# Hybrid attention layer: where the filler matmuls of the output projection start and stop, and when the first head's tiles are loaded

## The chip, the cores and the metric

One core of one Trainium2 chip runs the program. The metric is the device time of one launch in microseconds, the median over runs. Before the change three runs took 2358.67, 2354.69 and 2355.07 us, so the median is 2355.07 us. Lower is better.

## The reference

One layer with a learned prefix of 16 meta tokens ahead of 2048 tokens of width 1024 (2064 rows in all). A layer norm comes first. One input projection gives q, k and v of 16 heads of width 64, a forget logit per head, a gate for attention, a pool input and a gate for the pool branch. Attention is causal, with a bias from a running sum of log-sigmoids:

```python
log_f = jax.nn.log_sigmoid(f_logit + b_forget)
c = jnp.cumsum(log_f, axis=1)
s = q @ k.T * HEAD_DIM ** -0.5 + c[t] - c[s]
p = jax.nn.softmax(where(causal, s, -inf))
a = (p @ v) * jax.nn.silu(g_att)
p = multiscale_pool(u, w_pool, pool_scale) * jax.nn.silu(g_pool)
y = jnp.concatenate([a, p], axis=-1) @ w_out
out = layer_norm(ALPHA * x + y)
```

The output projection `w_out` has 2048 input rows, the first 1024 for the attention branch and the last 1024 for the pool branch, and 1024 output columns. The output drops the 16 meta rows. All of it is float32; the kernel gets the precision by splitting operands in a high and a low part and adding three products.

## The kernel before, in words

The program has three stages. In the first (lines 189 to 710) the rows are normalised, transposed and kept in SBUF, and a list of jobs (lines 657 to 668) projects them: `qk_job` for a head's q and k, `gp_job` and `u_job` for the pool branch, `ga_job` for the attention gate. A job makes its result in tiles, each of 24 matmuls (`proj`, line 490), in the two PSUM buffers of `dense` (line 169). `ga_job` (line 599) makes four tiles of 512 tokens; for each, ScalarE writes silu of the tile to `gst` (line 602), which has a single SBUF buffer, and a transfer stores it to `gd` in device memory. Everything but the last of these jobs runs before the attention pools are opened; the last one (`run_jobs(drain, len(jobs))`, line 796) is the `ga_job` of column block 7, and runs after they are opened.

The second stage is attention (lines 713 to 1103). The order of heads and query chunks is `seqn`: for each head the four chunks `j` of 512 queries, and for the last two heads the chunks 3, 0, 1, 2 in turn. Each (head, chunk) is cut in units: one per full key tile of 128 keys, and two more for the ragged end (`units`, line 895), so 3, 7, 11 and 15 units for the four chunks and 576 in all. The loop over `m` (lines 1080 to 1099) writes out, for each unit: `emit_s` (scores `s` on TensorE in one of four PSUM buffers; two exponentials on ScalarE, to `ph` in SBUF and back to `s`; pair sums `tu` and `acc` on GpSimd), then filler matmuls, then `emit_pl` (VectorE: `pl`, the low part of the exponential, and the running sum `acc`), and with a lag of four units `emit_pv` (products `xo` and `yo` with v). Each engine runs its instructions in the order in which they are written out here.

The filler is the output projection (`out_proj`, line 871): 32 tiles of the pool half, 16 with the first 512 output columns and 16 with the second, and then four `EARLY` tiles (12 to 15) of the attention half. Each tile is 24 matmuls `d<-wh,xm` and `d<-wl,xm` in one PSUM buffer (line 848), with its rows `xm` in one of two buffers. `out_tiles` is a generator that yields 1 after a matmul and 0 where it has to wait for something (line 835). Line 1079 gives the bounds: from unit `LEAD` = 24 to the last but `TAIL` = 24 the 768 matmuls of the pool half are spread over the units by weight; after that up to four are taken per unit. What is left then runs behind the loop (line 1100).

Every second unit calls `service` (line 1060): it takes one task of `wtasks`, which loads one of eight weight blocks (`wo_task`, line 825; `wst` has four buffers), and three rounds later splits it: `wh` on ScalarE, `wl` on VectorE (`wo_split`, line 814). It also runs the steps that are due for finished chunks (`chunk_end`, line 909: reciprocal, gate, store to `xa`).

The keys, values and queries come from device memory. `load_kv` (line 744) loads a quarter of a head's k and v in four transfers (`ka`, `kb`, `vt`, `vc`), `load_q` (line 760) a chunk of q in three (`qa` twice, `qb`). Ahead of the last job only the first quarter of head 0 and the first chunk are asked for (lines 792 to 795); `prefetch` (line 777) asks for the others from within the loop. All transfers are issued by SyncE, in one order that a scheduler sets; it may move a transfer ahead of others, and each waits at the head of the queue until its data and its buffer are free.

The third stage (lines 1105 to 1169) does the rest of the attention half of the projection and the closing layer norm, with its own buffers for the rows; the first two row tiles still come through the two `xm` buffers of the second stage (`first_x`, line 880).

Of the kernel before, what the change touches and what calls it, by code (L numbers as in the profile page):

```python
# [40 lines left out]
def kernel(  # L41
# [20 lines left out]
    nc = tc.nc  # L62
# [35 lines left out]
    nc = NC()  # L98
    mm = nc.tensor.matmul

    def dma(out, in_):
        out, in_ = out[tuple(slice(None) for _ in out.shape)], in_[tuple(slice(None) for _ in in_.shape)]
        nc.sync.dma_start(
            out.bitcast(F32) if out.dtype == F32R else out, in_.bitcast(F32) if in_.dtype == F32R else in_
        )
# [6 lines left out]
    def split(hi, lo, src, lo_eng=None):  # L112
        nc.scalar.copy(out=hi, in_=src)
        (lo_eng or nc.vector).tensor_tensor(out=lo, in0=src, in1=f32(hi), op=ALU.subtract)
# [18 lines left out]
    def pool(stack, name, **k):  # L133
        if k.get("space") is not DRAM:
            k["reuse_waits"] = "tile"
        return stack.enter_context(tc.tile_pool(name=name, bufs=1, **k))
# [535 lines left out]
    def fetch(n):  # L672
        return w_load(jobs[n][2]) if n < len(jobs) else None

    cur = w_first
    state = {"st": fetch(1)}
# [6 lines left out]
    def run_jobs(n0, n1):  # L683
        for n in range(n0, n1):
            fn, a, _ = jobs[n]

            def mid():
                if n + 1 < len(jobs):
                    state["w"] = w_split(state["st"])
                    state["st"] = fetch(n + 2)  # L690

            w = state.get("w") or cur
            if fn is not qk_job:
                m = n
                steps = 0
                while m < len(jobs) and jobs[m][0] is not qk_job and m != drain:
                    steps += 40 if jobs[m][0] is u_job else 32
                    m += 1
                sched["steps"] = steps if m == drain else steps + KT
                sched["tail"] = True  # L700
            fn(a, w, mid)
# [33 lines left out]
    NQ = 3  # L735
# [8 lines left out]
    def load_kv(h, i):  # L744
        ka, kb, (vt, vc) = kas[h % 2], kbs[h % 2], vts[h % 2]
        half, h8 = divmod(h, 8)
        if i == loaded[h]:
            loaded[h] += 1
            c0, c1 = 512 * i + (NM if i else 0), 512 * (i + 1) + NM
            dma(ka[2:68, c0:c1], kqd[h, 0:66, c0:c1])  # L750
            dma(kb[:, c0:c1], kqd[h, 2:130, c0:c1])
            dma(vt[:, 4 * i : 4 * i + 4, 0:P], vd[half][h8, :, 4 * i : 4 * i + 4, :])
            dma(vc[0:NM, i, 0:P], vd[half][h8, :NM, 4 * i + 4, :])
# [6 lines left out]
    def load_q(n):  # L760
        h, j = seqn[n]
        qa = qas[n % NQ]
        qb = kvs[0].tile([P, 512], F32R, tag="qb", name="qb", bufs=NQ)
        sl = slice(NM + 512 * j, NM + 512 * (j + 1))
        dma(qa[0:2, :], kqd[h, 258:260, sl])
        dma(qa[4:68, :], kqd[h, 194:258, sl])
        dma(qb, kqd[h, 130:258, sl])
        qt[n] = (qa, qb)
# [3 lines left out]
    kvq = deque()  # L772
    for n, (h, j) in enumerate(seqn):
        kvq.extend((h, i) for i in range(4) if i <= j and (h, i) not in kvq)
    fetched = [0]
# [13 lines left out]
            load_q(fetched[0])  # L789
            fetched[0] += 1  # L790

    load_kv(0, 0)
    load_q(0)
    fetched[0] = 1
    kvq.popleft()
    run_jobs(drain, len(jobs))
    phase_a.close()

# [1 line left out]
    bw = pool(phase_w, "bw", side="right")  # L800
# [8 lines left out]
    def wo_load(pl, half, n, k):  # L809
        st = pl.tile([P, 512], F32, tag="wst", name="wst", bufs=4)  # L810
        dma(st, wout[8 * half + k, :, 512 * n : 512 * (n + 1)])
        return st

    def wo_split(pl, half, n, k, st, eng=None):
        wh = pl.tile([P, 512], F32R, tag="wh", name="wh", bufs=KT)
        wl = pl.tile([P, 512], F32R, tag="wl", name="wl", bufs=KT)
        split(wh, wl, st, eng)
        wsl[half, n, k] = (wh, wl)
# [6 lines left out]
    def wo_task(args):  # L825
        def a():
            st = wo_load(bw, *args)
            todo_late.append((state["round"] + 3, lambda: wo_split(bw, *args, st, None)))

        return a  # L830

    wtasks = deque(wo_task((1, 0, k)) for k in range(KT))
    todo_late = deque()
# [221 lines left out]
                after(1, lambda: chunk_end(p, j))  # L1055

    total_fill = 2 * 16 * KT * 3
    nseq = len(seq)

    def service():  # L1060
        state["round"] += 1
        r = state["round"]
        while todo_late and todo_late[0][0] <= r:
            todo_late.popleft()[1]()
        if wtasks:
            wtasks.popleft()()
        due = sorted(t for t in post if t[0] <= r)
        for t in due:
            post.remove(t)
            t[2]()  # L1070
# [5 lines left out]
        n, i, u, nu = seq[m] if m < nseq else seq[-1]  # L1076
        return 2.0 if i < nu - 2 else 1.0

    LEAD, TAIL = 24, 24
    for m in range(nseq + LAG):  # L1080
        if m < nseq:
            emit_s(m)
        if m >= LEAD:
            if m < nseq - TAIL:
                w = [weight(t) for t in range(m, nseq - TAIL)]
                state["fill"] += (total_fill - filled[0]) * w[0] / sum(w)
            else:
                state["fill"] = 4.0
            k = min(int(state["fill"]), 4)
            state["fill"] = min(state["fill"] - k, 4.0)  # L1090
            fill(k)
        if m < nseq:
            emit_pl(m)
        if m >= LAG:
            emit_pv(m - LAG)
        if 0 < m < nseq:
            prefetch(seq[m][0], seq[max(m - LAG + 1, 0)][0])
        if m % 2:
            service()
    for r in filler:  # L1100
        if not r:
            service()
# [30 lines left out]
    for i in range(AHEAD - 1):  # L1133
        c_half(order[i], *tiles[i], 0)
        for k in range(KT * i // (AHEAD - 1), KT * (i + 1) // (AHEAD - 1)):
            wo_split(cp, 0, 1, k, sts[k])
            if k + WAHEAD < KT:
                sts.append(wo_load(bw, 0, 1, k + WAHEAD))
            service()
# [5 lines left out]
    for i, tt in enumerate(order):  # L1145
        if i + AHEAD < 16:
            c_half(order[i + AHEAD], *tiles[i + AHEAD], 0)
        xs, yt, st = tiles[i]
# [80 lines left out]
```

## Time and profile before

| what | value |
|---|---|
| median of three runs | 2355.07 us (2354.69 to 2358.67) |
| the profiled execution | 2353.42 us, span 2351.7 us, mean granted clock of TensorE 0.994 |
| TensorE matmuls | busy 2289.3 us (97%), 11450 instructions |
| VectorE, ScalarE, GpSimd | busy 1501.9, 959.9 and 716.8 us |
| first stage, attention, third stage | to 1320.45 us, to 2169.1 us, to the end |
| first and last filler matmul in the attention loop | at 1358.57 us and about 2167 us |

Times in the profile are counted from the start of the span. Busy time of TensorE holds matmuls that overlap: a 512-column matmul is listed with 0.39 us, but the next one starts 0.23 us after it when nothing waits. So a stretch in which TensorE lost time is seen better by the matmuls that it started per microsecond than by its busy share. Line L86 is a helper through which every instruction is recorded; the tile names tell the instructions apart.

### The profile page before, as it was taken

What the parts mean: (1) busy time and instruction counts of PE and PEld (TensorE: products, weight loads), DVE (VectorE), ACT (ScalarE), POOL (GpSimd) and SP (SyncE); (2) the same over time, 40 slices, a digit from 0 to 9 for tenths busy, and PEclk for the clock granted to TensorE, in tenths of its full rate; (3) what the DMA queues carried; (4) which work ended last, traced back from release to release, by engine and by line L of the source; (5) the groups of instructions that cost most, each with busy time, mean ns of one, the idle gap of its engine ahead of it and who ended that gap; (6) DMA issues with size and microseconds to landing.
All of it is one profiled execution on the core that took longest, in us unless ns stands there. A gap on an engine that the chain in (4) does not pass through costs nothing.

```text
span 2351.7 us, 32595 instructions
## 1 busy us (share of the span) xinstructions
PE 2289.3 (97%) x11450; PEld 1924.1 (82%) x11450; DVE 1501.9 (64%) x2372; ACT 959.9 (41%) x1813; POOL 716.8 (30%) x528
## 2 busy tenths in 40 slices
PE   6999999999999999999999999999999999998998
PEld 5878799999999999999888677777777777776787
DVE  6641146755766567656634488778788878877357
ACT  4431221212212212121111587777778777776000
POOL 4740021212313414140001235444453544444000
PEclk8999999999999999999999999999999999999999
DMA  7853222222222222222212857566666667555965
GB/s 252 265 175 90 69 90 70 84 63 92 91 62 91 78 70 91 62 95 80 82 65 71 219 170 226 162 210 175 186 189 187 208 173 228 169 164 164 300 193 165
DMA packets 317507, 333.59 MB, mean 142 GB/s; under 512 B 27744, under 2 KB 241072, under 8 KB 317312
## 3 DMA queue, kind: packets, MB, share of 16 engines
q1 hardware_dynamic: 317344, 331.51, 46.2%
q8 instruction: 91, 1.49, 0.3%
q14 instruction: 72, 0.59, 0.1%
HBM read 207.43 MB, written 124.00 MB: 141 GB/s over the span
## 4 chain that ended last, share of the span: by engine, by line
PE 89%; DVE 3%; DMA 3%; ACT 2%; issue 2%; POOL 1%; SPq 0%; DVEq 0%; ACTq 0%; POOLq 0%
PE d L86 61%; PE s L86 11%; PE yo L86 7%; PE mx L86 6%; PE xo L86 5%; POOL tu L86 1%; DVE pl L86 1%; PE tr L86 1%; ACT ph L86 1%; POOL araw L86 1%; DMA wst<-in_wout_dram 0%; ACT s L86 0%; DMA wu<-in_wut_dram 0%; DMA g_bc<-in_ln_in_g_dram 0%; DVE acc L86 0%
## 5 line engine op out<-in xcount | busy, mean ns | idle before, releaser
L86 PE MATMUL d<-hh,wh 128*128 128x412 f32 (+2 forms) x1472 | 543.8, 369 | 0.0
L86 PE MATMUL d<-hl,wh 128*128 128x412 f32 (+2 forms) x1472 | 538.2, 366 | 0.0
L86 PE MATMUL d<-hh,wl 128*128 128x412 f32 (+2 forms) x1472 | 537.9, 365 | 0.0
L86 DVE TENSOR_TENSOR pl<-s,ph 128x512 fp32r<-128x512 f32 (+2 forms) x576 | 375.4, 664 | 147.0 <-ACT s L86 134.2
L86 DVE TENSOR_REDUCE mxs<-mx 128x1 f32<-128x912 f32 (+14 forms) x416 | 359.5, 865 | 85.6 <-PE mx L86 75.8
L86 ACT ACTIVATE ph<-s 128x512 fp32r<-128x512 f32 (+2 forms) x576 | 335.2, 582 | 170.1 <-PE s L86 157.8
L86 PE MATMUL d<-wh,xm 128*128 128x512 f32 x1024 | 352.1, 400 | 4.5 <-DMA xm<-xa 3.7
L86 ACT ACTIVATE s<-s 128x512 f32<-128x512 f32 (+2 forms) x576 | 332.7, 578 | 0.0
L86 PEld LDWEIGHTS d<-hl,wh 128*128 128x128 f32 x1472 | 277.6, 189 | 24.8
L86 PEld LDWEIGHTS d<-hh,wh 128*128 128x128 f32 x1472 | 276.8, 188 | 23.2
L86 PEld LDWEIGHTS d<-hh,wl 128*128 128x128 f32 x1472 | 276.6, 188 | 23.4
L86 PE MATMUL s<-qa,ka 68*128 68x512 f32 (+4 forms) x704 | 257.9, 367 | 19.1 <-DVE pl L86 18.8
L86 POOL TENSOR_TENSOR wl<-wst,wh 128x1024 fp32r<-128x1024 f32 x40 | 96.3, 2407 | 571.4 <-ACT wh L86 545.8
L86 PE MATMUL s<-qb,kb 128*128 128x512 f32 (+4 forms) x704 | 244.8, 351 | 0.0
L86 PE MATMUL xo<-ph,vt 128*128 128x512 f32 (+3 forms) x640 | 232.7, 367 | 0.0
L86 POOL TENSOR_TENSOR tu<-ph 128x512 f32<-128x512 f32 x144 | 191.2, 1330 | 135.3 <-ACT ph L86 118.8
L86 PEld LDWEIGHTS d<-wh,xm 128*128 128x128 f32 x1024 | 192.3, 189 | 42.3 <-issue 2.9
L86 PE MATMUL yo<-pl,vt 128*66 128x512 f32 (+3 forms) x640 | 223.3, 365 | 1.1 <-ACT c L86 1.1
L86 PE MATMUL d<-wl,xm 128*128 128x512 f32 x512 | 204.3, 399 | 0.0
L86 PE MATMUL mx<-ka,qa 66*128 66x512 f32 (+5 forms) x704 | 197.9, 347 | 3.4 <-ACT qa L86 3.4
L86 PEld LDWEIGHTS s<-qa,ka 68*128 68x128 f32 (+1 forms) x704 | 127.8, 182 | 73.3 <-DVE pl L86 31.1
L86 DVE TENSOR_TENSOR mx<-mx,mask_q 128x128 f32<-128x128 f32 x256 | 76.6, 299 | 117.4 <-PE mx L86 115.0
(140 smaller groups left out, 3091.5 us busy)
## 6 DMA issues: line engine op xcount, KB each, us to landing
xm<-xp SPq DMA_DIRECT2D x32, 1024.0 KB
xm<-xa SPq DMA_DIRECT2D x20, 1024.0 KB
vd<-vs SPq DMA_DIRECT2D x32, 512.0 KB
vt<-vd SPq DMA_DIRECT2D x64, 256.0 KB
qb<-kqd SPq DMA_DIRECT2D x64, 256.0 KB
xa<-am SPq DMA_DIRECT2D x32, 512.0 KB
xp<-pm SPq DMA_DIRECT2D x32, 412.0 KB
kqd<-lo SPq DMA_DIRECT2D x64, 206.0 KB
```

Source lines behind the costliest of these rows:

```text
L86: return in_order(f(*a, **k))
```

## The change

Four edits. `LEAD` and `TAIL` go from 24 and 24 to 14 and 8. All four quarters of head 0 and the first three chunks of q (`NQ` is 3) are loaded ahead of the last projection job. In the first eight rounds of `service` two weight tasks are taken per round. The blocks that these tasks load are split two rounds later, with `wl` on GpSimd.

```diff
-    load_kv(0, 0)
-    load_q(0)
-    fetched[0] = 1
-    kvq.popleft()
+    for i in range(4):
+        load_kv(*kvq.popleft())
+        if i < NQ:
+            load_q(i)
+    fetched[0] = NQ
     run_jobs(drain, len(jobs))
     phase_a.close()
...
             st = wo_load(bw, *args)
-            todo_late.append((state["round"] + 3, lambda: wo_split(bw, *args, st, None)))
+            d, eng = (2, nc.gpsimd) if state["round"] < 8 else (3, None)
+            todo_late.append((state["round"] + d, lambda: wo_split(bw, *args, st, eng)))
...
     total_fill = 2 * 16 * KT * 3
+    LEAD, TAIL = 14, 8
     nseq = len(seq)
...
-        if wtasks:
-            wtasks.popleft()()
+        for _ in range(2 if r < 8 else 1):
+            if wtasks:
+                wtasks.popleft()()
...
-    LEAD, TAIL = 24, 24
     for m in range(nseq + LAG):
```

On SyncE, at the last projection job, the transfers stood like this before (`gd<-gst` is the store of a gate tile, the others are loads for attention):

```order
L86 DMA qa<-kqd 64x512
L86 DMA qb<-kqd 128x512
L86 DMA gd_68<-gst 128x512
L86 DMA ka<-kqd 66x512
L86 DMA kb<-kqd 128x512
L86 DMA vt<-vd_58 128x4x128
L86 DMA gd_68<-gst 128x512
L86 DMA vc<-vd_58 16x128
L86 DMA qa<-kqd 2x512
```

and now like this:

```order
L86 DMA qa<-kqd 64x512
L86 DMA qb<-kqd 128x512
L86 DMA ka<-kqd 66x512
L86 DMA kb<-kqd 128x512
L86 DMA vt<-vd_58 128x4x128
L86 DMA vc<-vd_58 16x128
L86 DMA gd_68<-gst 128x512 x3
L86 DMA wst<-in_wout_dram 128x512
L86 DMA gd_68<-gst 128x512
```

The first store of the job stood behind seven of the attention loads and now stands behind 25, and two more stores follow it directly.

On ScalarE, in the first units of attention, a weight cast (`wh<-wst`) stood between the exponentials (`ph`, `s`) of two units:

```order
L86 COPY c_10556<-yo 65x512
L86 ACTIVATE ph<-s 128x512
L86 ACTIVATE s<-s 128x512
L86 CAST wh<-wst 128x512
L86 ACTIVATE ph<-s 128x400
L86 ACTIVATE s<-s 128x400
L86 ACTIVATE ph<-s 128x432
L86 ACTIVATE s<-s 128x432
L86 CAST wh<-wst 128x512
```

and now two stand together, four times over:

```order
L86 COPY c_10578<-yo 65x512
L86 ACTIVATE ph<-s 128x512
L86 ACTIVATE s<-s 128x512
L86 CAST wh<-wst 128x512 x2
L86 ACTIVATE ph<-s 128x400
L86 ACTIVATE s<-s 128x400
L86 ACTIVATE ph<-s 128x432
L86 ACTIVATE s<-s 128x432
L86 CAST wh<-wst 128x512 x2
```

All eight casts now stand ahead of the exponentials of unit 12; before, three of them did.

On TensorE, behind the last score matmuls of attention, filler stood between the last products before (`d<-wh,xm` is a matmul of the first `EARLY` tile):

```order
L86 MATMUL s<-qa,ka 16x16
L86 MATMUL s<-qb,kb 16x16
L86 MATMUL d<-wh,xm 128x512 x2
L86 MATMUL d<-wl,xm 128x512
L86 MATMUL d<-wh,xm 128x512
L86 MATMUL xo<-ph,vt 128x512
L86 MATMUL yo<-pl,vt 66x512
L86 MATMUL d<-wh,xm 128x512
```

and now none does:

```order
L86 MATMUL s<-qa,ka 16x16
L86 MATMUL s<-qb,kb 16x16
L86 MATMUL xo<-ph,vt 128x512
L86 MATMUL yo<-pl,vt 66x512
L86 MATMUL xo<-ph,vt 128x512
L86 MATMUL yo<-pl,vt 66x512
L86 MATMUL xo<-ph,vt 128x512
L86 MATMUL yo<-ph,zo 66x512
```

All four `EARLY` tiles now stand behind the last product of attention, where three stood. The pool half of the filler now ends at unit 567 of 575. Before, it ended at unit 552, the units 553 to 572 had no filler, and the first `EARLY` tile began at unit 573.

## Rows read from the trace of the kernel before

**Rows 1.** The page: busy time of TensorE; the chain that ended last, by engine.

```profile
PE 2289.3 (97%) x11450; PEld 1924.1 (82%) x11450; DVE 1501.9 (64%) x2372; ACT 959.9 (41%) x1813; POOL 716.8 (30%) x528
PE 89%; DVE 3%; DMA 3%; ACT 2%; issue 2%; POOL 1%; SPq 0%; DVEq 0%; ACTq 0%; POOLq 0%
```

**Rows 2.** Windows: length, busy us (instructions) by engine, TensorE clock, DMA share, GB/s.

```profile
1301.00:1313.00 12.00, 12.00 (x53) 9.76 (x52) 0.27 (x1) 1.20 (x2) 3.84 (x5) 1.00 0.83 226
1320.45:1358.57 38.12, 32.40 (x162) 22.66 (x160) 29.18 (x47) 33.76 (x67) 11.36 (x11) 0.91 0.96 262
1325.50:1332.30 6.80, 4.93 (x18) 3.68 (x17) 3.26 (x5) 5.82 (x12) 1.71 (x2) 0.50 1.02 276
1344.18:1358.57 14.39, 12.69 (x64) 8.31 (x62) 13.65 (x23) 14.39 (x30) 5.13 (x4) 1.00 0.86 249
1400.00:1700.00 300.00, 296.80 (x1576) 228.41 (x1575) 244.30 (x380) 232.91 (x445) 139.09 (x106) 1.00 0.64 190
2126.50:2158.00 31.50, 25.37 (x124) 18.00 (x123) 30.47 (x45) 25.37 (x51) 16.35 (x12) 0.95 0.69 200
2169.00:2190.75 21.75, 17.24 (x76) 13.35 (x74) 3.56 (x6) 2.67 (x5) 0.00 (x0) 1.00 0.90 268
2190.75:2340.00 149.25, 149.25 (x658) 123.57 (x659) 84.84 (x124) 8.18 (x20) 4.28 (x3) 1.00 0.71 224
```

**Rows 3.** Timeline of ScalarE, last job to unit 1: start, length, idle before, releaser.

```profile
1304.01 0.60 ACT L86 ACTIVATE gst<-d 128x512 f32<-128x512 f32 x1 [4.54 <-PE d L86]
1309.73 0.60 ACT L86 ACTIVATE gst<-d 128x512 f32<-128x512 f32 x1 [5.12 <-DMA gd<-gst]
1315.13 0.60 ACT L86 ACTIVATE gst<-d 128x512 f32<-128x512 f32 x1 [4.80 <-PE d L86]
1320.69 0.60 ACT L86 ACTIVATE gst<-d 128x512 f32<-128x512 f32 x1 [4.96 <-PE d L86]
1321.31 1.28 ACT L86 ACT_TABLE_LOAD   x1
...
1326.46 0.50 ACT L86 ACTIVATE ph<-s 128x400 fp32r<-128x400 f32 x1 [2.77 <-DMA gd<-gst]
```

**Rows 4.** Timeline of SyncE's queue: when a transfer was issued.

```profile
1301.12 0.37 SPq L86 DMA_DIRECT2D ka<-kqd  x1
...
1304.87 0.37 SPq L86 DMA_DIRECT2D gd<-gst  x1
...
1321.32 0.32 SPq L86 DMA_DIRECT2D gd<-gst  x1
...
2126.64 0.56 SPq L86 DMA_DIRECT2D rd<-st  x1
...
2129.05 1.27 SPq L86 DMA_DIRECT2D rb<-rd  x2
...
2175.95 0.57 SPq L86 DMA_DIRECT2D xm<-xa  x1
```

**Rows 5.** Chain of waits: pieces that are transfers (start, length).

```profile
1321.32 5.04 DMA gd<-gst
1327.34 4.56 DMA ka<-kqd
```

**Rows 6.** Timeline of ScalarE, first units of attention.

```profile
1328.14 0.60 ACT L86 ACTIVATE ph<-s 128x512 fp32r<-128x512 f32 x1
...
1329.13 0.61 ACT L86 ACTIVATE ph<-s 128x512 fp32r<-128x512 f32 x1
...
1342.99 0.62 ACT L86 CAST wh<-wst 128x512 fp32r<-128x512 f32 x1 [1.00 <-DMA wst<-in_wout_dram]
1343.51 0.59 ACT L86 ACTIVATE ph<-s 128x512 fp32r<-128x512 f32 x1
```

**Rows 7.** Timeline of TensorE: starts after a wait, and a gap.

```profile
1328.02 0.79 PE L86 MATMUL s<-qa,ka 68*128 68x512 f32 x1 [1.87 <-DVE pl L86]
...
2183.76 0.47 PE L86 MATMUL d<-wh,xm 128*128 128x512 f32 x1 [2.46 <-DMA xm<-xa]
```

## The prediction

> **What bounds the kernel now.** I read the page first: TensorE is listed busy for 97% of the span and holds 89% of the chain that ended last [rows 1]. So the time is TensorE's work, which the change does not alter (the same matmuls, in another order), plus the time in which TensorE waits. Then I read windows, to find where it waits. In the middle of attention it starts 1576 matmuls in 300 us, 5.25 per us; in the third stage, where all are 512 columns wide, 658 in 149.25 us, 4.41 per us [rows 2]. At these rates the other stretches show what they lose:
>
> - From the first score matmul to the first filler (1320.45 to 1358.57) there are 162 matmuls in 38.12 us. They need 162 / 5.25 = 30.9 us, so 7.3 us are lost. ScalarE is busy for 33.8 of them, and for all of the last 14.39 us [rows 2]: two exponentials per unit hold it for about 1.0 us (a pair begins at 1328.14, the next at 1329.13 [rows 6]), a full unit's four matmuls hold TensorE for 0.93.
> - From 2126.5 to 2158 (the units 553 to 572, which have no filler) there are 124 matmuls in 31.5 us; they need 23.6, so 7.9 are lost. VectorE is busy for 30.5 of them [rows 2].
> - From 2169.00 to 2190.75 three early tiles stand alone: 72 filler matmuls need 72 / 4.41 = 16.3 us of 21.75, so 5.4 are lost [rows 2], in waits for `xm` and the single accumulator (2.46 us is the longest [rows 7]).
>
> The sum of these, 20.6 us, is all that the change can win back; the rest of attention is bound by TensorE at either density of filler. Next I read ScalarE and SyncE's queue at the last projection job, because the change fills that queue [rows 3, 4].
>
> **The change part by part.** The sum is made against the profiled execution, 2353.42 us, which is 1.65 below the median of the runs, 2355.07.
>
> *Loads ahead of the last job's stores.* Before, seven loads took SyncE from 1301.12 to 1304.87, and the first gate store followed at once [rows 4]. It landed at 1309.73, 4.86 us later, when ScalarE could write `gst` again [rows 3]. Now 25 loads go first. The first seven take 3.75 us. Beyond eight, a transfer waits until the eighth before it has landed: the one issued at 1327.34 took 4.56 us and held the queue for that time [rows 5], so eight go per 4.56 us, 0.57 each. That puts the store at 1301.12 + 3.75 + 18 x 0.57 = 1315.1, landing 5 us later at 1320.1. The second silu comes with it, instead of at 1309.73. TensorE's fourth tile needs that silu's PSUM buffer: it starts at 1320.7 instead of about 1315.1, a wait of 5.6 us that did not exist. The tile itself takes 5.5 us (silus at 1315.13 and 1320.69 [rows 3]).
>
> The clock then counts. After the stretch with little work before 1328.02, TensorE was granted half its clock (0.50, that is 1.2 of 2.4 GHz) from 1325.5 to 1332.3 [rows 2, 7], of which 4.3 us lie behind the resumption and cost 2.1; after the lone gap of 2.46 us the window shows 1.00 [rows 2, 7]. My gap of 5.6 us is nearer to the first case, so I add 2.1 (bounds 0 and 5.5, the tile wholly at half). The Trainium skill (page "TensorE: Matmul & The Clock Gate", section on the clock gate) says that the array falls to the lower of its two levels when it has been idle, which speaks against this change. By that rule the fourth tile pays; the 2.46 us gap shows that not every gap does, and without the charge the sum below is 2.1 lower.
>
> So the last tile ends at 1320.7 + 5.5 + 2.1 = 1328.3 instead of 1320.6. The fourth silu follows there (the chain of stores 2 and 3 fits: two stores of 3.5 us and two silus of 0.6 after 1320.7 end at 1328.9). Unit 1's exponential waited for the last store before, until 1326.46 [rows 3], 5.04 us after its issue [rows 5]. With fewer loads ahead of it I take 3.5 us; nothing shows a lone store of this size, so the ends are 2.4 (the small store at 2126.64, whose reader was issued at 2129.05 [rows 4]) and 5.04. It starts at 1328.9 + 0.6 + 3.5 = 1333.0: **+6.5 us** for ScalarE's run of exponentials (bounds 0, if the first store lands in 2.4, all others too and the clock holds, and +10.5, if each of four takes 5.04).
>
> *Weights by twos.* Eight casts instead of three stand in the exponentials of units 1 to 12, 0.5 us each (1342.99 to 1343.51 [rows 6]): 5 x 0.5 = +2.5. The wait of 1.00 us for a weight block [rows 6] goes: -1.0. Moving `wl` to GpSimd costs nothing while GpSimd has slack (busy 11.4 of 38 us [rows 2]); without it VectorE's running sum comes late, which I bound at 1 us. Net **+1.5** (0.5 to 2.5).
>
> *Filler from unit 14.* After its first idle yields it starts at unit 17 instead of 27. Units 17 to 27 took 14.39 us with 64 matmuls, 12.2 at the middle rate [rows 2]; some 15 filler matmuls of 0.23 us come in, 15.7 in all: +1.3 there, and -3.5 later, where they are missing and TensorE is the bound: **-2.2**.
>
> *Filler to unit 567.* Of the 20 bare units, 8 remain, and ScalarE enters them without arrears, since the units ahead of them carry four filler matmuls each. It needs 8 x 1.0 + 5 casts x 0.5 + 0.5 = 11 us for them, VectorE about 2.5 more for the last sum and `pl`; TensorE's own work to the end of attention is about 11.3 us. That loses 2.2, and 3.5 with some of the slowing that VectorE showed before. Instead of 7.9: **-4.4** (-6 to 0).
>
> *A fourth tile behind attention.* Its matmuls only move. Each tile's `xm` is asked for when the tile two ahead has ended; the one asked for at 2175.95 let TensorE go on at 2183.76, 7.8 us later [rows 4, 7], against 5.5 us of work. With one more tile in that chain: **+1** (-1 to +3).
>
> Together: 6.5 + 1.5 - 2.2 - 4.4 + 1 = +2.4, so 2355.8 by the profiled execution's own time and 2357.5 by the median; I forecast 2357. From no change a measurement of this kernel can tell about 0.2%, 4.7 us, so this is no change. The ends, each term at its bound, are 0 + 0.5 - 2.2 - 6 - 1 = -8.7 and 10.5 + 2.5 - 2.2 + 0 + 3 = +13.8.
>
> **The rivals.**
>
> *A. Slower, by the queue.* The mechanism is the first term at its upper end: every store lands in about 5 us, so that the fourth silu waits for the third store rather than for TensorE, and the half clock lasts through the whole tile. It decides when the fourth silu starts behind about 1331. Then the first term is +10.5 and, with a tail that gives 3 to 4, the sum is 10.5 + 1.5 - 2.2 - 3.5 + 1 = +7.3: about 2362. For it: 4.86 and 5.04 us are the only landings of this store that the trace shows [rows 3, 5], and the loads move more bytes in this time than before, when the share of the DMA engines was already 0.83 [rows 2]. Against: stores 2 to 4 find almost no loads ahead of them.
>
> *B. Faster, by the tail and an early start.* The loads drain sooner, the first store lands near 1317.5, TensorE waits about 2.5 us and keeps its clock as after the 2.46 us gap [rows 7]. Unit 1 then starts 1 to 2 us late: 1.5 + 1.5 - 2.2 = +0.8 at the start, and the tail gives all it can, -6: about -5 to -6, 2350. For it: GB/s reached 262 to 276 in windows with more transfers in flight [rows 2]. Against: at 0.5 us each, the 25 issues alone last until 1314.
>
> *C. The moves do not happen.* If a scheduler put the stores ahead of the loads again, the start would gain about 3 instead of losing 6, and the sum be near -7: 2348. The order on SyncE's queue speaks against it.
>
> **How the numbers follow.** The forecast's case has 0.48, A 0.31, B 0.17, C 0.04. Its own range is 2352 to 2361. To leave out no more than 2 in 10, the range goes into A up to 2365 and into B down to 2349. Faster by over 0.2% is B and C, 0.21; within 0.2% is the forecast's case, 0.48; slower is A, 0.31.
>
> **What would show it.** In the profile after: ScalarE's second `gst` of the last job begins near 1320 and is released by the store of `gd`; TensorE has a gap of about 5 us ahead of the job's fourth tile, with a granted clock under 1 behind it; unit 1's exponential starts near 1333; the first `d<-wh,xm` comes at unit 17, about 33 us after the first score matmul; the bare units at the end lose under 4 us; and attention ends near 2165 (2169.1, plus 1.4 by the first four terms, less 24 x 0.23 for the early tile that no longer stands in it). I am wrong if that gap is missing or over 8 us, or if the end of attention still loses 8 us.

## The result, and the profile after

| | median | runs | against before |
|---|---|---|---|
| before | 2355.23 us | 8 (2354.30 to 2358.67) | |
| after | 2364.85 us | 8 (2361.27 to 2367.42) | 1.0037, 95% interval 1.0028 to 1.0046 |

The change costs 9.6 us, 0.41% by the medians (the 1.0037 in the table is the ratio of the means). The forecast was 2357; 2364.85 lies at the very edge of the range, 0.15 us inside it. The profiled execution took 2366.80 us with a span of 2365.0, against 2353.42 and 2351.7.

The page of the changed kernel, as [rows 1]: TensorE's work is as before, so the 13.3 us are waits and clock.

```profile
PE 2295.9 (97%) x11450; PEld 1929.7 (82%) x11450; DVE 1493.4 (63%) x2364; ACT 962.0 (41%) x1813; POOL 727.7 (31%) x536
PE 89%; DMA 4%; DVE 2%; issue 2%; POOL 1%; ACT 1%; SPq 0%; POOLq 0%; DVEq 0%; ACTq 0%
```

Windows of the changed kernel, with the columns of [rows 2]: first score matmul to first filler; ten microseconds of that; the middle; the end of attention without filler; the four early tiles; the first tile of the third stage.

```profile
1329.73:1360.64 30.91, 22.82 (x102) 15.68 (x101) 15.71 (x24) 23.84 (x46) 17.43 (x16) 0.83 0.87 250
1349.73:1359.73 10.00, 9.08 (x27) 6.24 (x26) 6.93 (x11) 8.66 (x17) 8.94 (x7) 0.50 0.78 236
1400.00:1700.00 300.00, 297.35 (x1577) 228.76 (x1577) 245.09 (x384) 235.79 (x449) 140.52 (x107) 1.00 0.63 187
2155.00:2170.62 15.62, 13.44 (x69) 8.78 (x69) 15.17 (x23) 11.47 (x23) 7.49 (x5) 0.95 0.66 206
2170.62:2202.52 31.90, 25.32 (x99) 19.53 (x97) 6.86 (x13) 2.86 (x5) 5.12 (x4) 0.92 0.81 245
2202.52:2210.00 7.48, 7.48 (x26) 5.99 (x27) 0.08 (x1) 1.24 (x2) 0.00 (x0) 0.77 1.16 316
```

The middle starts the same 5.25 matmuls per us. From the first score to the first filler 102 matmuls need 19.4 us at that rate and take 30.9: 11.5 lost, where 7.3 were. Before, ScalarE was busy for the whole end of this stretch; now it is busy for 23.8 of 30.9 us, so it waits itself. The bare end lost 7.9; 2155.00 to 2170.62 loses 15.62 - 69 / 5.25 = 2.5. The early tiles lost 5.4; their 96 matmuls now need 21.8 and take 31.9, so 10.1 are lost.

ScalarE's timeline, as [rows 3, 6], then SyncE's queue, as [rows 4], then TensorE's starts after a wait, as [rows 7], all of the changed kernel:

```profile
1304.79 0.60 ACT L86 ACTIVATE gst<-d 128x512 f32<-128x512 f32 x1 [4.54 <-PE d L86]
1321.94 0.60 ACT L86 ACTIVATE gst<-d 128x512 f32<-128x512 f32 x1 [16.56 <-DMA gd<-gst]
1325.07 0.60 ACT L86 ACTIVATE gst<-d 128x512 f32<-128x512 f32 x1 [2.53 <-DMA gd<-gst]
1329.98 0.60 ACT L86 ACTIVATE gst<-d 128x512 f32<-128x512 f32 x1 [4.31 <-PE d L86]
...
1333.58 0.50 ACT L86 ACTIVATE ph<-s 128x400 fp32r<-128x400 f32 x1 [0.61 <-DMA gd<-gst]
...
1345.96 0.62 ACT L86 CAST wh<-wst 128x512 fp32r<-128x512 f32 x1 [4.10 <-DMA wst<-in_wout_dram]
```

```profile
1317.41 8.61 SPq L86 DMA_DIRECT2D gd<-gst  x3
...
1330.97 0.42 SPq L86 DMA_DIRECT2D wst<-in_wout_dram  x1
...
1341.54 1.25 SPq L86 DMA_DIRECT2D wst<-in_wout_dram  x2
```

```profile
1322.60 0.79 PE L86 MATMUL d<-hh,wh 128*128 128x512 f32 x1 [6.78 <-ACT gst L86]
...
1340.94 0.45 PE L86 MATMUL yo<-pl,vt 128*66 128x512 f32 x1 [2.36 <-ACT c L86]
...
1348.98 0.50 PE L86 MATMUL s<-qa,ka 68*128 68x512 f32 x1 [3.29 <-DVE pl L86]
...
2184.86 0.47 PE L86 MATMUL d<-wh,xm 128*128 128x512 f32 x1 [0.90 <-DMA xm<-xa]
...
2192.88 0.77 PE L86 MATMUL d<-wh,xm 128*128 128x512 f32 x1 [2.29 <-DMA xm<-xa]
...
2202.52 0.50 PE L86 MATMUL d<-wh,xm 128*128 128x512 f32 x1 [2.33 <-DMA xm<-xa]
```

Two new waits stand at the start. The forecast one: the second silu at 1321.94, behind the store issued at 1317.41, and TensorE's 6.78 us for it. The other was not forecast: ScalarE stands for 4.10 us, because weight blocks 3 and 4 were issued only at 1341.54, ten microseconds after block 2 and behind the loads of head 1. TensorE waits 3.29 us behind it and then has half its clock for ten microseconds (the second window). At the end three tiles wait for `xm`.

### The profile page after: what moved, and what is told of

Read it like the earlier page. It is cut to its first block, busy times and chain, and to the rows that moved or that the text cites. A ratio compares the mean times of both kernels' runs of the same rounds, so it can differ in the third digit from the quotient of the medians.

```text
span 2365.0 us, 32586 instructions
## 1 busy us (share of the span) xinstructions
PE 2295.9 (97%) x11450; PEld 1929.7 (82%) x11450; DVE 1493.4 (63%) x2364; ACT 962.0 (41%) x1813; POOL 727.7 (31%) x536
## 4 chain that ended last, share of the span: by engine, by line
PE 89%; DMA 4%; DVE 2%; issue 2%; POOL 1%; ACT 1%; SPq 0%; POOLq 0%; DVEq 0%; ACTq 0%
PE d L86 59%; PE s L86 12%; PE yo L86 8%; PE mx L86 6%; PE xo L86 5%; PE tr L86 1%; DVE pl L86 0%; DMA vt<-vd 0%; DMA wst<-in_wout_dram 0%; DMA wu<-in_wut_dram 0%; SPq L86 0%; DMA xt<-in_x_dram 0%; POOL araw L86 0%; DVE acc L86 0%; DMA xm<-xa 0%
## 5 line engine op out<-in xcount | busy, mean ns | idle before, releaser
L86 POOL TENSOR_TENSOR wl<-wst,wh 128x1024 fp32r<-128x1024 f32 (+1 forms) x48 | 106.7, 2227 | 577.6 <-ACT wh L86 550.8
```

What stands on the lines that cost most here:

```text
L86: return in_order(f(*a, **k))
```

## The experiments

All runs are medians against runs of before on the same chip (2355.24 to 2355.55). To see where a kernel gains or loses I cut its profiled execution at landmarks: the first silu of the last job, the last score matmul (the one with 16 columns) of the chunks number 6, 30, 42 and 60, of 64 in the order of `seqn` and counted from 0, the first matmul of the third stage, the end. Each stretch is compared with before, less 0.227 us (1 / 4.41) for every filler matmul that it has more. Each row is one execution: the one of e5 is 3.1 us under that kernel's median, the others within 2 us, so the stretches tell where, and the medians how much.

| against before, us | start, to chunk 6 | to 30 | 30 to 42 | to 60 | to the third stage | third stage |
|---|---|---|---|---|---|---|
| after | +12.3 | -0.6 | -2.0 | +1.4 | -0.1 | +1.6 |
| tail alone (e2) | -0.9 | -0.1 | -3.9 | -0.7 | +0.3 | +1.5 |
| tail, twos (e5) | +5.4 | -0.2 | -4.0 | -0.7 | -1.5 | 0.0 |
| tail, twos, LEAD (e1) | +4.7 | -0.6 | -0.7 | +1.5 | +0.2 | +1.5 |
| tail, loads (e6) | +8.0 | -0.3 | -3.7 | -0.8 | -0.7 | 0.0 |
| tail, LEAD (e12) | -1.2 | -0.3 | -1.2 | +0.1 | +0.2 | +1.2 |

**The changed kernel without the early loads (e1).** The diff's first hunk is undone:

```diff
-    for i in range(4):
-        load_kv(*kvq.popleft())
-        if i < NQ:
-            load_q(i)
-    fetched[0] = NQ
+    load_kv(0, 0)
+    load_q(0)
+    fetched[0] = 1
+    kvq.popleft()
```

> The changed kernel with the loads put back as before: one quarter of head 0 and one chunk of q ahead of the last projection job. Theory 1 (the early loads cost the start directly: the first gate store stands behind 25 loads, TensorE waits 6.8 us for the second silu and then runs at half clock): the silu starts about 5 us after the first, the gap in TensorE goes, unit 1's exponential starts 6 to 7 us earlier relative to the job's start; but the other quarters of head 0 now stand ahead of weight blocks 3 and 4 in SyncE's queue, so ScalarE's wait for them stays or grows by 1 to 3 us. Time 2359 to 2361 (2364.85 less 4 to 6). Theory 2 (the start is bound by the bytes to be moved, whoever asks first): what the job gains the first units lose, 2364 to 2366.

2360.41 us, 1.0019 (1.0010 to 1.0027): 4.4 less than the change, as theory 1 has it. The gap in TensorE is gone. ScalarE's wait for weights is not, though it shrank from 4.10 us, where theory 1 had it stay or grow:

```profile
1342.44 0.62 ACT L86 CAST wh<-wst 128x512 fp32r<-128x512 f32 x1 [2.78 <-DMA wst<-in_wout_dram]
```

So without its best suspect the change is still slower than before.

**The tail alone (e2).**

```diff
-    LEAD, TAIL = 24, 24
+    LEAD, TAIL = 24, 8
```

> The kernel before with TAIL 8 in place of 24 and nothing else. Theory 1 (the prediction's step for the fourth early tile was too small: the bare units win 4 to 5 us, but the four early tiles with their late weights and rows lose 5 to 6 us behind attention): 2355 to 2358, no gain against 2355.23, and three waits for xm behind attention with the clock at one half after them. Theory 2 (all that the change loses is lost at the start, the tail gives -4.4 + 1 as the prediction had it): 2351 to 2352.5.

2350.04 us, 0.9975 (0.9965 to 0.9985): 1 us below theory 2's range and far below theory 1's, and neither has the place. In the table the gain stands between chunks 30 and 42 (-3.9); at the end (+0.3 and +1.5) what the bare units give is lost again. Two waits for `xm` of the kind that theory 1 named are there, on TensorE:

```profile
2176.11 0.47 PE L86 MATMUL d<-wh,xm 128*128 128x512 f32 x1 [2.71 <-DMA xm<-xa]
...
2184.66 0.80 PE L86 MATMUL d<-wh,xm 128*128 128x512 f32 x1 [2.83 <-DMA xm<-xa]
```

**The last chunk's steps later (e3).**

```diff
-                after(1, lambda: chunk_end(p, j))
+                after(9 if n == NB - 1 else 1, lambda: chunk_end(p, j))
```

> The changed kernel, with the steps for the last finished chunk (reciprocal, gate, store to xa) begun eight rounds later. Theory 1 (in the changed kernel the rounds for the early tiles' weights come in a burst behind the loop and pull these steps along, so that SyncE's queue holds the loads of xm behind the last chunk's store at 2193.36, and VectorE's yt stands behind its reciprocal): the yt wait of 1.07 us and most of the xm waits of 0.90, 2.29 and 2.33 us go, with some of the half clock behind them: 2364.85 less 3 to 5, so 2360 to 2362. Theory 2 (each xm takes 7.3 us to load against 5.5 us of matmuls, so the waits are the loads' own): within 1 us of the changed kernel, 2364 to 2366.

2368.20 us, 1.0049 (1.0037 to 1.0062): slower by 3.4, a miss for both. The first waits shrank (the 0.90 went, 2.29 became 1.47), but the steps moved on to a worse place. The chain of waits of this kernel:

```profile
2193.50 4.32 DMA rd<-st
...
2200.34 8.65 DMA xm<-xa
2208.99 0.14 issue
2209.13 6.01 PE d L86 x14
```

SyncE issued `rb` behind the store of `rd`, and an `xm` only behind that; TensorE waited 5.46 us at 2209.13. Shifting a step along one in-order queue moves the wait to the next load in it.

**Head 1 later (e4).**

```diff
-            if h >= 2 and last_use[h - 2] >= nv or (k and not near) or first_use[h] > n + 5:
+            if h >= 2 and last_use[h - 2] >= nv or (k and not near) or first_use[h] > n + (1 if n < 4 else 5):
```

> The changed kernel, with the loads of head 1 asked for from unit 21 instead of from unit 1, so that no load of head 1 stands ahead of a weight block. Theory 1 (ScalarE's idle stretch of 4.10 us at 1341.9, behind which TensorE waits 3.29 us and then runs at half clock to 1360, is the wait for weight blocks 3 and 4 behind 14 loads on SyncE's queue): the stretch goes, the first filler matmul comes 4 to 7 us earlier relative to the first score matmul, 2364.85 less 4 to 6: 2359 to 2361. Theory 2 (the blocks would be late by the bytes alone, or blocks 5 to 8 and the two xm loads bring the same wait one pair later): the first filler matmul comes at the same distance, 2364 to 2366.

2363.74 us, 1.0034 (1.0022 to 1.0046): 1.1 under the change, too little to tell. The first filler matmul comes 3.0 us earlier relative to the first score matmul (27.95 us against 30.91), less than theory 1 asked. The 4.10 us wait did go, so the loads of head 1 caused it; but the next pair waits (ScalarE), and TensorE does too:

```profile
1346.96 1.27 ACT L86 CAST wh<-wst 128x512 fp32r<-128x512 f32 x2 [1.24 <-DMA wst<-in_wout_dram]
```

```profile
1353.81 0.49 PE L86 MATMUL yo<-pl,vt 128*66 128x512 f32 x1 [1.76 <-ACT c L86]
```

**Weights by twos on the tail alone (e5).** The kernel of e2 with the hunks in `wo_task` and `service`:

```diff
+            d, eng = (2, nc.gpsimd) if state["round"] < 8 else (3, None)
+            todo_late.append((state["round"] + d, lambda: wo_split(bw, *args, st, eng)))
...
+        for _ in range(2 if r < 8 else 1):
```

> TAIL 8 and the weights by twos with wl on GpSimd; LEAD stays 24 and the loads stay as before. It stands between the tail alone (2350.04) and the changed kernel without the early loads (2360.41), which has LEAD 14 in addition. Theory 1 (the weights by twos are the loss: pairs of casts wait for blocks whose buffers GpSimd's slow wl frees late, ScalarE stands still, TensorE idles about 4 us and then runs at half clock): 2356 to 2360, with ScalarE waiting 2 to 4 us for wst about 20 us after the first score matmul. Theory 2 (the loss is the early filler of LEAD 14, which adds 0.47 us of matmuls to units that are bound by ScalarE or run at half clock): 2350 to 2352, little worse than the tail alone.

2355.35 us, 0.9999 (0.9990 to 1.0008): 5.3 over the tail alone, with the loss at the start in the table (+5.4 against -0.9). Theory 1 has the place, and the time is just under its range:

```profile
1344.16 0.62 ACT L86 CAST wh<-wst 128x512 fp32r<-128x512 f32 x1 [3.16 <-DMA wst<-in_wout_dram]
```

**The same with `wl` on VectorE (e10).**

```diff
-            d, eng = (2, nc.gpsimd) if state["round"] < 8 else (3, None)
+            d, eng = (2, None) if state["round"] < 8 else (3, None)
```

> As the run with TAIL 8 and the weights by twos (2355.35), but wl on VectorE instead of GpSimd. Theory 1 (GpSimd takes 1.25 us for each wl and frees the four wst buffers late, so blocks 5 to 8 are asked for late and ScalarE waits for the last pair 3.16 us): with 0.7 us each the buffers are free 1 to 3 us earlier, the wait shrinks, 2351 to 2353. Theory 2 (four buffers and a landing of 4 to 5 us cannot feed two casts per two units, whoever makes wl; the pairs themselves are the cost): 2354 to 2357.

2356.18 us, 1.0007 (0.9998 to 1.0015): theory 2. ScalarE waits even more, so GpSimd is not to blame:

```profile
1338.78 1.36 ACT L86 CAST wh<-wst 128x512 fp32r<-128x512 f32 x2 [2.39 <-DMA wst<-in_wout_dram]
...
1345.38 1.36 ACT L86 CAST wh<-wst 128x512 fp32r<-128x512 f32 x2 [3.25 <-DMA wst<-in_wout_dram]
```

**The early loads on the tail alone (e6).** The kernel of e2 with the first hunk:

```diff
-    load_kv(0, 0)
-    load_q(0)
...
+    for i in range(4):
+        load_kv(*kvq.popleft())
...
```

> TAIL 8 and the early loads of head 0 alone; weights one per round, LEAD 24. Theory 1 (the early loads cost by themselves, by the late gate stores: 6.5 us as the prediction had it, 4.4 as the changed kernel without them showed): 2354 to 2357 against 2350.04 for the tail alone. Theory 2 (the cost of the loads comes only together with the weights by twos, since alone they take the rest of head 0 out of the first units' queue, ahead of the weight blocks): 2349 to 2352.

2356.86 us, 1.0010 (1.0001 to 1.0019): 6.8 over the tail alone, theory 1. The loads cost by themselves.

**A free buffer for the gate tiles (e9).** The changed kernel; the second and third silu of the last job write to the weight tile, which is free by then.

```diff
-            st = wq.tile([P, 512], F32, tag="gst", name="gst")
+            if c < 7 or j in (0, 3):
+                st = wq.tile([P, 512], F32, tag="gst", name="gst")
+            else:
+                if j == 1:
+                    sp = wq.tile([P, KT, P], F32, tag="wst", name="wst")
+                    sp = sp.rearrange("p a b -> p (a b)")
+                st = sp[:, 512 * (j - 1) : 512 * j]
```

> The changed kernel, loads still first, but the second and third gate tile of the last job go to the free weight tile instead of waiting for the single gst buffer. Theory 1 (the early loads cost because the second silu waits for the first store behind them, and TensorE for that silu): the gap of 6.78 us ahead of the job's fourth tile and the half clock behind it go, attention starts 7 to 9 us earlier; the last store still ends late, so that 4 to 6 us are left: 2359 to 2361 against 2364.85, about what the changed kernel without the early loads takes (2360.41). Theory 2 (the early loads cost by the bytes they take from the first units): 2363 to 2366.

2357.26 us, 1.0008 (0.9999 to 1.0017): 7.6 under the change, theory 1, and more than it asked. ScalarE:

```profile
1310.56 0.60 ACT L86 ACTIVATE wst<-d 128x512 f32<-128x512 f32 x1 [4.97 <-PE d L86]
...
1325.23 0.50 ACT L86 ACTIVATE ph<-s 128x400 fp32r<-128x400 f32 x1 [0.57 <-DMA gd<-gst]
...
1336.88 0.62 ACT L86 CAST wh<-wst 128x512 fp32r<-128x512 f32 x1 [3.37 <-DMA wst<-in_wout_dram]
```

The second silu now waits for TensorE alone, and unit 1 starts 8.4 us earlier (1325.23 against 1333.58). The wait for weights stays.

**LEAD alone on the tail (e12).** In the kernel before:

```diff
-    LEAD, TAIL = 24, 24
+    LEAD, TAIL = 14, 8
```

> TAIL 8 and LEAD 14, with the loads and the weights (one per round) as before. The weights are not there before unit 27, so no filler can come early; what LEAD 14 alters is the spread: how much filler each later unit takes. Theory 1 (LEAD 14 costs by the early filler in units 17 to 27): 2349 to 2351, as the tail alone (2350.04). Theory 2 (it costs by the spread, which lets filler fall where VectorE is late, the waits of 0.4 to 1.5 us for pl between 1780 and 2060 that the run with weights by twos alone does not have): 2352 to 2355.

2353.44 us, 0.9993 (0.9984 to 1.0001): 3.4 over the tail alone, with no loss at the start, so theory 2. The place is where the filler pauses for the second set of weights (no filler matmul from 1773.2 to 1790.8 in e2, from 1772.3 to 1787.8 here). Windows of the tail alone and of this kernel:

```profile
1765.00:1800.00 35.00, 34.32 (x186) 26.12 (x186) 33.04 (x52) 31.85 (x64) 11.87 (x10) 1.00 0.74 230
```

```profile
1765.00:1800.00 35.00, 33.30 (x177) 24.54 (x175) 32.34 (x50) 29.96 (x60) 12.27 (x9) 1.00 0.78 231
```

There it starts nine matmuls fewer, with VectorE busy for 32 to 33 of 35 us in both. Between chunks 30 and 42 TensorE's waits for `pl` add up to 4.3 us in the kernel before, 0.8 in e2 and 3.4 here. The two bounds together fix on which units the pause falls; that this place is the cause is argued from these rows, and why one place costs 3 us more than another was not tried.

**The weight casts on GpSimd (e7).** TAIL 8; `wh` of the pool half by GpSimd.

```diff
+        if half:
+            nc.gpsimd.tensor_copy(out=wh, in_=st)
+            nc.vector.tensor_tensor(out=wl, in0=st, in1=f32(wh), op=ALU.subtract)
+        else:
+            split(wh, wl, st, eng)
```

> TAIL 8, weights one per round as before, but the eight (and later eight) casts wh of the pool half go from ScalarE to GpSimd, wl stays on VectorE. Theory 1 (the first 27 units are bound by ScalarE, so that eight casts of 0.5 us out of it shorten them): 2350.04 less 2 to 4, so 2346 to 2348, and the first filler matmul 33 to 35 us after the first score matmul instead of 37.2. Theory 2 (GpSimd's casts of about 1.3 us hold its pair sums back, VectorE's running sum waits, and the gain is eaten): 2349 to 2353.

2353.05 us, 0.9992 (0.9983 to 1.0000): 3.0 over the tail alone, a miss for theory 1, and the time of theory 2 without its reason: GpSimd's casts are quick (timeline, 1.17 us for two). ScalarE falls to 20.75 of 27.50 us (window of this kernel), and VectorE stays at 26.18. The tail alone, at the same distance from the job's first silu (last window), has VectorE as full, 26.84, beside ScalarE's 26.65: so these units were not bound by ScalarE alone, and taking work from it could not shorten them. Why they took longer is not shown.

```profile
1332.89 1.17 POOL L86 CAST wh<-wst 128x512 fp32r<-128x512 f32 x2
```

```profile
1333.50:1361.00 27.50, 23.68 (x115) 16.58 (x115) 26.18 (x41) 20.75 (x40) 13.19 (x14) 0.93 0.81 226
```

```profile
1332.23:1359.73 27.50, 25.35 (x131) 18.27 (x130) 26.84 (x45) 26.65 (x55) 9.94 (x8) 1.00 0.88 247
```

**Two more buffers for the early tiles (e8).** TAIL 8; the third and fourth early tile's rows go to tiles of head 14, which is done.

```diff
+        if half == 0 and i in (2, 3):
+            t = kbs[0] if i == 2 else vts[0][0].rearrange("p a b -> p (a b)")
+            t = t[:, 0:2048].rearrange("p (k a b) -> p k a b", k=8, a=2)
+        else:
+            t = pl.tile([P, 8, 2, P], F32R, tag="xm", name="xm", bufs=bufs)
...
```

> TAIL 8, and the rows of the third and fourth early tile go to the key and value tiles of the finished head 14 instead of waiting for one of the two xm buffers. Theory 1 (behind attention TensorE waits for xm because each load of about 7.5 us can only be asked for when the tile two ahead has ended; the waits of 2.71 and 2.83 us and the half clock behind them go): 2350.04 less 4 to 6, so 2344 to 2346. Theory 2 (the loads are bound by the DMA engines, which are 0.85 to 0.9 busy there, or hold the weight blocks of the early tiles back): a gain under 1 us, or a loss to 2352.

2344.03 us, 0.9957 (0.9944 to 0.9969): theory 1, 6.0 under the tail alone and 11.2 under before. No wait for `xm` is left on TensorE behind attention:

```profile
2162.54 0.50 PE L86 MATMUL d<-wh,xm 128*128 128x512 f32 x1 [0.78 <-DVE yt L86]
2169.05 0.50 PE L86 MATMUL d<-wh,kb 128*128 128x512 f32 x1 [0.78 <-DVE yt L86]
2175.69 0.51 PE L86 MATMUL d<-wh,vt 128*128 128x512 f32 x1 [0.78 <-DVE yt L86]
```

**The last gate store off the path (e11).** As e8, with the gate tiles of e9, but the second and fourth in the weight tile, so that unit 1's `ph` does not lie where the last store reads.

> TAIL 8 and the tail's rows in the tiles of head 14 (2344.03), and in the last job the second and fourth gate tile in the free weight tile; loads, weights and LEAD as before. Theory 1 (unit 1's exponential waits 2.8 us for the fourth store only because its ph lies where gst lay; the units behind it are bound by ScalarE, so the wait goes in full, with some of the half clock behind it): 2340 to 2342, with unit 1's exponential 1 us behind unit 0's. Theory 2 (the next thing is as late: head 0's loads or the first weight block hold the units): 2343 to 2345.

2344.57 us, 0.9956 (0.9942 to 0.9970): theory 2. Unit 1's wait went, and ScalarE waits for the next two weight blocks instead, 4.13 us in all, where in e8 it waited 2.24 for the store and 1.46 for a block:

```profile
1337.27 0.62 ACT L86 CAST wh<-wst 128x512 fp32r<-128x512 f32 x1 [1.72 <-DMA wst<-in_wout_dram]
...
1342.78 0.62 ACT L86 CAST wh<-wst 128x512 fp32r<-128x512 f32 x1 [2.41 <-DMA wst<-in_wout_dram]
```

## Why the prediction was right or wrong

From the tail alone the parts add up in the order e2, e5, e1, after: -5.2 (tail), +5.3 (twos), +5.1 (LEAD), +4.4 (loads) is +9.6. The prediction had -3.4, +1.5, -2.2 and +6.5, so the first and the last were out by about 2 us each, and the two in the middle, which are the steps that failed, by 3.8 and 7.3. That 2364.85 still lies in the range is luck: the range went up to 2365 only to take in rival A, and A's mechanism did not decide.

- *Loads ahead of the stores, +6.5: right.* First store issued at 1317.41 (forecast 1315.1), second silu 1321.94 (1320.1), TensorE's gap 6.78 us (5.6), clock 0.50 behind it, unit 1's exponential 6.3 us later than before, counted from the job's first silu. The runs give 4.4 (on top of the rest) and 6.8 (alone); e9 shows the mechanism.
- *Weights by twos, +1.5: wrong, the first step that failed.* I struck out the 1.00 us wait for a block ("-1.0") and counted only casts. The wait grew to 4.10 us, and e5 prices the edit at 5.3. Asking sooner did bring the blocks sooner, but by less than the casts were moved: counted from the job's first silu, the last block was issued at 35.9 us in e5 and at 39.9 in e2, and the last cast began at 41.1 and at 47.8. All casts now stand ahead of the exponentials of unit 12, so ScalarE, in order, stands in front of blocks that are not there. The DMA engines, listed at 0.96 before [rows 2], are at 1.05 in the first 27.44 us of attention in e5 (1320.36 to 1347.80); that this fullness is what holds the blocks back is argued, not shown. I had looked past the queue at the job's stores only, and not at what stands ahead of the weights in it.
- *Filler from unit 14, -2.2: wrong, the second step that failed, and the larger.* It stood at -2.2 at both ends of the sum, without a bound. At the start it gave 0.7 (e1 against e5). I took the later units as bound by TensorE, wherever filler falls; they are not: between chunks 30 and 42 e1 stands 3.3 behind e5, and to chunk 60 another 2.2. Alone it costs 3.4 (e12).
- *Filler to unit 567, -4.4, and the fourth early tile, +1: the sum was nearly right, by two errors.* The bare stretch lost 2.5 as forecast (2.2 to 3.5). The chain of `xm` loads cost 4.7 more than before (10.1 against 5.4), and part of the third stage's first tile ran at half clock besides (+1.6 in the table), not +1. The end as a whole gave nothing; most of the 5.2 that TAIL 8 gained (e2) stands at the pause in the middle, which I had at nothing.
- *The rivals.* The time is near rival A's 2362, but its mechanism did not decide: the fourth silu began at 1329.98, ahead of A's 1331, and was released by TensorE, not by a store. B and C are out. Of the signs named, the late silu, the gap and its clock, unit 1 near 1333 and the bare units under 4 us came; attention ended at 2170.6, not 2165, and the first filler came 30.9 us after the first score matmul (forecast 33), which itself stood 8.5 us later than before.

## What to carry to other kernels

Before a load or a cast is asked for sooner, look at what stands ahead of it on its queue and whether the DMA engines are full there: if so, the data may come sooner by less than it is read sooner, and an in-order engine that reads it early just waits early. A wait for a buffer goes by another buffer, best one that is idle already: a few lines that reused finished tiles were worth 6.0 us (e8) and 7.6 us (e9), but nothing where the next wait took the place of the one that went (e11); and shifting the order of steps (e3, e4) only moved the wait. Price the edits of a change one by one: here three losses hid a gain.

## What the runs showed of the hardware that was not expected

After its 6.78 us gap TensorE was back at full clock within 3.4 us of the resumption (0.52 from 1322.60 to 1326.00, 1.00 after). After the 3.29 us wait that ended at 1348.98 the clock stayed at 1.00 until 1349.73 and was then 0.50 until 1359.98, for 10.25 us, though TensorE was busy for 9.33 of them (the second window shows ten). So the longer gap had the shorter stretch at half clock behind it. The Trainium skill (page "TensorE: Matmul & The Clock Gate", section "HAM oscillation — how this bites in real kernels") describes a kernel whose clock falls back at each wait for a transfer between bursts of matmuls. Here not every wait did that: the one of 2.36 us left the clock at 1.00 (1340.94 to 1345.69), and no run here shows why it stayed down so long after the next. GpSimd cast a 128 x 512 block in about 0.58 us (1.17 for two), less than half of the 1.25 us that its subtraction of the same size takes (2.49 to 2.52 for two `wl` in the changed kernel).
